# Trading places: stick-breaking branch products and the first mixer gate, with per-item rates for the weight sums

## The chip, the cores and the metric

The kernel runs on one core of one Trainium2 chip. The metric is the device time of one execution in microseconds (us). Before the change the median of 3 runs is 1070.77 us (1067.01 to 1071.44). A separate execution was recorded by the hardware profiler. The engines are PE (matrix products), PEld (its weight loads), DVE (vector engine), ACT (scalar engine), POOL (GpSimd, which here mostly issues DMAs) and SP (which issues the loads of weights).

## The reference

One decoder layer on x of 512 tokens by 1024 channels, in float32:

```python
proj = x @ w_in                      # q, k, v of three attentions, and three gates of 1024 channels
o_da = diff_attention(...)           # 4 heads, two softmax maps per head, RMSNorm per head
o_sb = stick_breaking_attention(...) # 8 heads of 64
o_dl = dilated_attention(...)        # 3 groups x 4 heads of 128
g = jax.nn.sigmoid(gates)            # 3 x 1024
merged = (g[:, :, 0] * (o_da @ w_branch_da) + g[:, :, 1] * (o_sb @ w_branch_sb)
          + g[:, :, 2] * (o_dl @ w_branch_dil))
x = layer_norm(alpha * x + merged @ w_out)
c = jnp.square(relu(x @ w_up)) @ w_down
ple = jax.nn.sigmoid(x @ w_ple_gate) * (p @ w_ple)
x = layer_norm(alpha * x + c + ple)
```

Only the order of the work around `merged`, and the time at which sums of weights are formed, are touched by the change.

## The kernel before, in words

**Products.** Every float32 operand is split into a rounded high part and a low part (fp32r), and a product is three matmuls: high x high, high x low, low x high. Some large products follow a scheme with seven products of half blocks in place of eight (`seven`, L541; `value_pair`). It needs sums and differences of blocks on both sides. Those of the activations are called forms here: `value_forms` (L343) loads x transposed again as eight `xr` tiles through POOL (L347) and makes the forms for the dilated values on DVE and ACT; `mixer_forms` (L507) makes those for the gates. Those of the weights are made by DMAs alone.

**Weights.** They are streamed in chunks of 128 x 1024 floats (512 KB): SP loads a `raw` tile (a ring of 7), ACT casts it to `wh` (L212), DVE subtracts to get `wl` (L214; rings of 6). `pump` (L220) does this a few chunks ahead of the item that uses them.

**Items.** `trunk` builds a list of 298 items in program order. An item is a group of matmuls (`mm`) into one bank of the matrix accumulator, with an evacuation (`ev`) that is issued one item later, and a `size` (a full item is a product of 128 rows by 512 with eight blocks, a half item half of that). A bank is one of two `mm` banks or one of six `at` banks. Items 1 to 64 are projections: q and k tiles ("T" items), values, and the seven-product items of `value_pair` (33 to 46). After that:

| items, before | what |
| --- | --- |
| 65 to 78 | `gate_alone(0, 1)`: gate of the stick-breaking branch, 14 half items |
| 79 to 86 | `branch_items(1)`: o_sb @ w_branch_sb, 8 half items |
| 87 to 100 | `gate_chain(1, 2)`: gate of the dilated branch |
| 101 to 108 | `branch_items(2)` |
| 109 to 122 | `gate_chain(2, 0)`: gate of the differential branch |
| 123 to 134 | `branch_items(0)`, with items that transpose `merged` between them |
| 135 to 297 | output projection, first norm, embedding, MLP (from about 173), second norm |

In a branch item a `pre` function, run one item ahead, puts the sigmoid on the gate (`gate_sig`, L495, ACT at L499); the evacuation multiplies the product by it on DVE (L651) and for branch 1 keeps the result as `merged`, for the others adds it to `merged` (L655).

**The loop** (L1816 and following) walks the items. For each it may add a generator to `pending`, may drain (L1827: ahead of item `branch_at[1] - 1`, which is 78, it steps all attention generators to their end), splits the heads' outputs two items ahead of a branch (`split_oT`, after stepping until the heads are ready), issues the previous item's evacuation, pumps weights, adds credit for sums, runs `pre`, calls `step()` and issues the matmuls.

`step()` advances the attention generators: eight `sb_head`, four `dil_head` (score products L1672, softmax over tables, a combination with L1721, transposes L1740), and sixteen `da_block(head, query block)`. A `da_block` does two score products, a softmax on ACT and DVE (L1583 to L1595), lets three steps pass, transposes (L1600), copies (`wT`, L98), and multiplies with the values (L1614). The last block of a head then normalizes (a power on POOL, `on` at L1627) and transposes once more (L1633). The bias tables of `da_block` are loaded by POOL (L1364) and copied by DVE (L1374).

**Weight sums.** 200 steps of 512 KB each combine blocks of weights in DRAM: a copy (L970) or an accumulating DMA (L968), all in POOL's queue, up to four sums taken in turn. Each step is made to wait for the weight split that was issued last. How many steps an item issues is set by a credit: 2.6 times the item's size for items 12 to 64, 1.4 times for 65 to 128, and 0.42 per item from 166 on (`RATES`). SP later loads the sums as weights.

Of the kernel before, what the change touches and what calls it, by code (L numbers as in the profile page):

```python
# [55 lines left out]
def trunk(tc, a, out):  # L56
    nc = tc.nc
    es = ExitStack()
    with es:
# [170 lines left out]
        items = []  # L230
# [164 lines left out]
        def value_pair(nv):  # L395


            v_from[0] = len(items) - 4
            cs, s, x = {}, {}, {}
            w = [a["wv"][nv + n, c].rearrange("p k n -> p (k n)") for n in range(2) for c in range(4)]  # L400

            for p in (2, 1, 7, 6, 4, 5, 3):
                for r in range(2):
                    if not r:
                        blk = {1: 0, 2: 2, 4: 6}.get(p)
                        cs[p] = [chunk(vsum[kp][{5: 0, 6: 1, 7: 2, 3: 3}[p]] if blk is None else w[blk + kp], 1024)
                                 for kp in range(2)]

                    def bank(p=p, r=r):
                        if p == 5:  # L410
                            x[r] = at_bank()
                        return x[r] if p in (5, 3) else at_bank() if r else mm_bank()

                    def mm(ps, p=p, r=r):
                        for k in range(4):
                            c = cs[p][k // 2]
                            n = slice(k % 2 * 512, k % 2 * 512 + 512)
                            h, lo = vf[p][k][r]
                            go, end = k == 0 and p != 3, k == 3 and p != 5
                            nc.tensor.matmul(ps, h, c["h"][:, n], start=go, stop=False, skip_group_check=True)  # L420
                            nc.tensor.matmul(ps, h, c["l"][:, n], start=False, stop=False, skip_group_check=True)
                            nc.tensor.matmul(ps, lo, c["h"][:, n], start=False, stop=end, skip_group_check=True)

                    def ev(ps, p=p, r=r):
                        if p in (2, 7):
                            s[p, r] = slot("dl_v")
                            nc.scalar.copy(s[p, r], ps)
                        elif p == 1:
                            s[1, r] = slot("dl_v")
                            nc.vector.tensor_add(s[2, r], s[2, r], ps)  # L430
                            nc.scalar.copy(s[1, r], ps)
                            V["dl_v", 1, r] = s[2, r]
                        elif p == 6:
                            nc.vector.tensor_add(s[1, r], s[1, r], ps)
                            nc.vector.tensor_add(s[7, r], s[7, r], s[1, r])
                        elif p == 3:
                            nc.vector.tensor_add(s[1, r], s[1, r], ps)
                            V["dl_v", 1, 2 + r] = s[1, r]
                        else:
                            o = V["dl_v", 2, r + 2 * (p == 5)] = slot("dl_v") if p == 4 else s[7, r]  # L440
                            nc.vector.scalar_tensor_tensor(o, s[7, r], -1.0, ps, op0=OP.mult, op1=OP.subtract)
                    item(cs[p] if r else [], mm, ev, need=cs[p], bank=bank, size=0.5)

        def v_items(nv, name, g):
            cs = [chunk(a["wv"][nv, c].rearrange("p k n -> p (k n)"), 1024) for c in range(4)]
            for tt in range(4):
                def mm(ps, tt=tt):
                    for k in range(8):
                        c = cs[k // 2]
                        s = slice((k % 2) * 512, (k % 2) * 512 + 512)  # L450
                        x1, x2 = xh[k][:, tt * P:tt * P + P], xl[k][:, tt * P:tt * P + P]
                        nc.tensor.matmul(ps, x1, c["h"][:, s], start=k == 0, stop=False)  # L452
                        nc.tensor.matmul(ps, x1, c["l"][:, s], start=False, stop=False)
                        nc.tensor.matmul(ps, x2, c["h"][:, s], start=False, stop=k == 7)  # L454
                        if k == 3:
                            yield

                def ev(ps, tt=tt):
                    if name == "sb_v":
                        v = [slot(name, F32R).rearrange("p (h two d) -> p h two d", two=2, d=64) for _ in range(2)]  # L460
                        pv = ps.rearrange("p (h d) -> p h d", d=64)
                        for i in range(2):
                            hs = slice(4 * i, 4 * i + 4)
                            nc.scalar.copy(v[i][:, :, 0, :], pv[:, hs, :])
                            nc.vector.tensor_sub(v[i][:, :, 1, :], pv[:, hs, :], v[i][:, :, 0, :].bitcast(F32))
                        V[name, g, tt] = v
                    else:
                        t = slot(name)
                        cp(t, ps)
                        V[name, g, tt] = t  # L470
                item(cs if tt == 3 else [], mm, ev, need=cs)

        nt, nv = 2, 0
        order = main_order()
# [15 lines left out]
        merged = {}  # L490
# [46 lines left out]
        def seven(forms, operand, bank_of, done):  # L537

            cs = {}
            for p in (2, 1, 7, 6, 4, 5, 3):  # L540
                for r in range(2):  # L541
# [19 lines left out]
                    if p == 5:  # L561
                        bank_of.get("sums", set()).add(len(items))
                    item(cs[p] if r else [], mm, ev, need=cs[p], bank=bank, size=0.5)

        msum = [[[dram.tile([P, 1024], F32, name=f"msum{n}_{m}_{i}") for i in range(4)] for m in range(2)]
                for n in range(3)]
# [67 lines left out]
        def branch_items(i, behind=()):  # L634
            behind = list(behind)
            for half in range(2):
                cs = [chunk(a["wb"][i, half, c].rearrange("p k n -> p (k n)"), 1024) for c in range(2)]
                for tt in range(4):
                    def mm(ps, tt=tt, cs=cs):
                        q = slice(tt * P, tt * P + P)  # L640
                        for k in range(4):
                            c = cs[k // 2]
                            n = slice(k % 2 * 512, k % 2 * 512 + 512)
                            h, lo = oTs[4 * i + k]
                            nc.tensor.matmul(ps, h[:, q], c["h"][:, n], start=k == 0, stop=False)  # L645
                            nc.tensor.matmul(ps, h[:, q], c["l"][:, n], start=False, stop=False)  # L646
                            nc.tensor.matmul(ps, lo[:, q], c["h"][:, n], start=False, stop=k == 3)  # L647

                    def ev(ps, tt=tt, half=half):
                        g = sg.pop((i, tt, half))  # L650
                        nc.vector.tensor_mul(g, g, ps)  # L651
                        if i == 1:
                            merged[tt, half] = g
                        else:
                            nc.vector.tensor_add(merged[tt, half], merged[tt, half], g)  # L655

                    def pre(tt=tt, half=half):
                        sg[i, tt, half] = gate_sig(i, tt, half)
                    item(cs if tt == 3 else [], mm, ev, need=cs, bank=at_bank, size=0.5)
                    items[-1]["pre"] = pre  # L660
                    if half and behind:
                        behind.pop(0)()

# [12 lines left out]
            item([], mm, ev, size=0.08)  # L676

        last_plain = len(items)
        gate_alone(0, 1)
        branch_at = {1: len(items)}  # L680
        branch_items(1)
        for n, i in ((1, 2), (2, 0)):
            gate_chain(n, i)
            branch_at[i] = len(items)
            branch_items(i, () if i else [lambda k=k: turn_item(k) for k in range(4)])

# [254 lines left out]
        def sum_steps():  # L941
# [34 lines left out]
            todo = deque(up_steps(vsum[m], [w[2 + i // 2, i % 2 * 2 + m] for i in range(4)], True) for m in range(2))  # L976
            todo.extend(up_steps(msum[n][m], a["wgm"][n, m]) for n in range(3) for m in range(2))
            todo.extend(up_steps(gsum[m], a["wg"][m]) for m in range(2))
            for m in range(ND):
                todo.append(up_steps(usum[m], a["wu"][m]))  # L980
                if m < ND - 1:
                    todo.append(down_steps(m))
            run = []
            while todo or run:
                while todo and len(run) < 4:
                    run.append(todo.popleft())
                for g in list(run):
                    s = next(g, None)
# [824 lines left out]

        DA_TABS = 44
        sum_steps_ = sum_steps()
        RATES = 2.6, 1.4  # L1816
        credit = 0.0
        plain_left[0] = last_plain
        forms_at = last_plain - 5
        freed = 8  # L1820
        prev = None
        for n, it in enumerate(items):
            if n == v_from[0]:
                pending.append(value_forms())
            if n == forms_at:
                pending.append(mixer_forms())
            if n == branch_at[1] - 1:  # L1827
                while active or waiting:
                    step()
            for i in range(3):  # L1830
# [25 lines left out]
            if n == 13:  # L1856
                pending.append(tables())

            if 12 <= n < wout_at - 6:
                credit += it["size"] * (RATES[0] if n < last_plain else RATES[1])  # L1860
            elif n > ple_at + 14:
                credit += 0.42
            while credit >= 1:
                credit -= 1
                next(sum_steps_, None)
# [139 lines left out]
```

## Time and profile before

| quantity | value |
| --- | --- |
| median of the runs shown | 1070.77 us (1067.01 to 1071.44, 3 runs) |
| the profiled execution's own time | 1073.48 us |
| its span in the trace | 1071.8 us |
| mean granted clock of PE over the span | 0.987 |
| HBM read, written | 251.21 MB, 106.98 MB |
| instructions | 15018 |

"Busy" is the share of the span in which an engine executed an instruction. A window is a stretch of the span, in us from its start; PEclk is the clock that PE was granted in it, as a part of full speed; GB/s is what the DMA engines moved. A row of the timeline is: start in us, duration in us, engine, line and operation, output and inputs with their shapes, how many instructions of the kind stand together, and, in brackets, the idle time ahead of it on its engine with the instruction that ended that. A row of the waits names the waiting engine and line, the instruction waited for, and then the total in us, the count and the longest.

### The profile page before, as it was taken

Reading aid. Unit: us, or ns where it says so; the run is one execution under the profiler, and the core shown is the slowest. Engines: PE = TensorE matmul, PEld = TensorE weight load, DVE = VectorE, ACT = ScalarE, POOL = GpSimd, SP = SyncE. Lnnn points to the kernel's source line nnn. Section 1 sums busy time; section 2 is a strip of 40 time slices with the busy share of each in tenths; the row PEclk is TensorE's granted clock in tenths of the full one; section 3 lists DMA queues with packets and bytes.
Section 4 is the critical chain, followed back from the end, with each engine's and each line's share of the span. In section 5 each row is a group of like instructions: output and inputs, shape, how many; then the busy total and the mean of one; then the engine's idle time right before and its main releaser. Section 6 shows DMA issues by size and latency. Waiting matters only on the chain.

```text
span 1071.8 us, 15018 instructions
## 1 busy us (share of the span) xinstructions
PE 1046.1 (98%) x5474; PEld 889.5 (83%) x5474; DVE 764.1 (71%) x1352; ACT 576.8 (54%) x982; POOL 179.5 (17%) x271
## 2 busy tenths in 40 slices
PE   9999999999999999898999999999999999999997
PEld 6887788878888788786888888888999989989885
DVE  6887667639864656985466664789677867877976
ACT  6675445426434544665362633585656565566741
POOL 0002322332322433021121130000111010100000
PEclk9999999998999999898999999999999999999999
DMA  8348987998999999387599993248999879857612
GB/s 312 112 168 252 230 266 204 289 311 241 362 270 256 321 267 321 115 252 266 153 289 302 320 348 101 79 125 299 262 313 285 288 220 288 270 182 240 195 41 79
DMA packets 72761, 254.32 MB, mean 237 GB/s; under 512 B 8968, under 2 KB 9880, under 8 KB 72688
## 3 DMA queue, kind: packets, MB, share of 16 engines
q0 software_dynamic: 32464, 116.21, 41.1%
q1 hardware_dynamic: 39648, 136.24, 36.4%
q8 instruction: 43, 0.70, 0.2%
q10 hardware_dynamic: 576, 0.92, 0.2%
q14 instruction: 30, 0.25, 0.1%
HBM read 251.21 MB, written 106.98 MB: 334 GB/s over the span
## 4 chain that ended last, share of the span: by engine, by line
PE 82%; DMA 10%; DVE 5%; issue 1%; ACT 1%; POOL 0%; DVEq 0%; SPq 0%; POOLq 0%; ACTq 0%
PE mm L87 8%; PE mm L89 8%; PE mm L88 8%; PE at L1131 4%; PE at L1132 4%; PE at L1133 4%; DMA msum<-in_wgm_dram 4%; PE at L552 3%; PE at L553 3%; PE at L554 3%; PE at L645 2%; PE at L646 2%; PE at L647 2%; DMA msum<-msum 2%; PE mm L452 2%; PE mm L454 2%
## 5 line engine op out<-in xcount | busy, mean ns | idle before, releaser
L214 DVE TENSOR_TENSOR wl<-raw,wh 128x1024 fp32r<-128x1024 f32 x251 | 305.5, 1223 | 135.8 <-ACT wh L212 133.6
L212 ACT CAST wh<-raw 128x1024 fp32r<-128x1024 f32 x251 | 263.3, 1051 | 253.9 <-PE mm L88 123.5
L87 PE MATMUL mm<-xhT,wh 128*128 128x512 f32 x304 | 121.1, 398 | 1.0 <-DVE da_qb L101 1.0
L89 PE MATMUL mm<-xhT,wl 128*128 128x512 f32 x304 | 119.2, 392 | 0.1
L88 PE MATMUL mm<-xlT,wh 128*128 128x512 f32 x304 | 118.9, 391 | 0.0
L1131 PE MATMUL at<-wh,hh 128*128 128x512 f32 x188 | 73.7, 392 | 0.0
L1132 PE MATMUL at<-wl,hh 128*128 128x512 f32 x188 | 73.7, 392 | 0.0
L87 PE MATMUL mm<-x1hT,wh 128*128 128x256 f32 x256 | 73.6, 288 | 0.0
L1133 PE MATMUL at<-wh,hl 128*128 128x512 f32 x188 | 73.1, 389 | 0.0
L88 PE MATMUL mm<-x1lT,wh 128*128 128x256 f32 x256 | 72.3, 283 | 0.0
L89 PE MATMUL mm<-x1hT,wl 128*128 128x256 f32 x256 | 71.8, 283 | 0.0
L87 PEld LDWEIGHTS mm<-xhT,wh 128*128 128x128 f32 x304 | 57.2, 188 | 12.7 <-PE at L1600 1.2
L89 PEld LDWEIGHTS mm<-xhT,wl 128*128 128x128 f32 x304 | 57.1, 188 | 12.6 <-DVE wl L214 0.5
L88 PEld LDWEIGHTS mm<-xlT,wh 128*128 128x128 f32 x304 | 57.1, 188 | 10.4
L87 PEld LDWEIGHTS mm<-x1hT,wh 128*128 128x128 f32 x256 | 48.8, 191 | 4.7 <-ACT up L1065 3.0
L88 PEld LDWEIGHTS mm<-x1lT,wh 128*128 128x128 f32 x256 | 48.8, 191 | 1.5
L968 POOL DMA_DIRECT2D usum<-in_wu_dram x32 | 27.8, 868 | 127.4 <-DVE wl L214 102.2
L89 PEld LDWEIGHTS mm<-x1hT,wl 128*128 128x128 f32 x256 | 48.6, 191 | 0.0
L1133 PEld LDWEIGHTS at<-wh,hl 128*128 128x128 f32 x188 | 35.3, 188 | 7.7
L1131 PEld LDWEIGHTS at<-wh,hh 128*128 128x128 f32 x188 | 35.5, 189 | 6.0
L1132 PEld LDWEIGHTS at<-wl,hh 128*128 128x128 f32 x188 | 35.5, 189 | 5.5
L968 POOL DMA_DIRECT2D dsum<-in_wd_dram x28 | 24.8, 886 | 86.4 <-DVE wl L214 72.0
(554 smaller groups left out, 2679.5 us busy)
## 6 DMA issues: line engine op xcount, KB each, us to landing
usum<-in_wu_dram POOLq DMA_DIRECT2D x48, 512.0 KB, 9.6
dsum<-in_wd_dram POOLq DMA_DIRECT2D x42, 512.0 KB, 10.6
raw<-in_wt_dram SPq DMA_DIRECT2D x38, 512.0 KB, 7.8
msum<-in_wgm_dram POOLq DMA_DIRECT2D x36, 512.0 KB, 14.2
raw<-usum SPq DMA_DIRECT2D x32, 512.0 KB, 5.3
raw<-dsum SPq DMA_DIRECT2D x28, 512.0 KB, 5.2
raw<-in_wd_dram SPq DMA_DIRECT2D x25, 512.0 KB, 4.5
raw<-msum SPq DMA_DIRECT2D x24, 512.0 KB, 7.7
```

The lines of the kernel that those rows point to most:

```text
L87: nc.tensor.matmul(ps, wh, xh, start=start, stop=False, skip_group_check=True)
L88: nc.tensor.matmul(ps, wh, xl, start=False, stop=False, skip_group_check=True)
L89: nc.tensor.matmul(ps, wl, xh, start=False, stop=stop, skip_group_check=True)
L212: i = nc.scalar.copy(h, raw)
L214: i = nc.vector.tensor_sub(lo, raw, h.bitcast(F32))
L552: nc.tensor.matmul(ps, h[:, q], c["h"][:, n], start=go, stop=False, skip_group_check=True)
L553: nc.tensor.matmul(ps, h[:, q], c["l"][:, n], start=False, stop=False, skip_group_check=True)
L554: nc.tensor.matmul(ps, lo[:, q], c["h"][:, n], start=False, stop=end, skip_group_check=True)
L968: i = nc.gpsimd.dma_start(o, i, accum_op=OP.add, max_dma_last_dim=4096)
L1131: nc.tensor.matmul(ps, h[:, q], c["h"][:, s], start=go, stop=False, skip_group_check=True)
L1132: nc.tensor.matmul(ps, h[:, q], c["l"][:, s], start=False, stop=False, skip_group_check=True)
L1133: nc.tensor.matmul(ps, lo[:, q], c["h"][:, s], start=False, stop=end, skip_group_check=True)
```

## The change

1. `branch_items(1)` comes ahead of `gate_alone(0, 1)`: items 65 to 72 are the branch products, 73 to 86 the gate. The branch items of branch 1 use an `mm` bank, have no `pre`, and their evacuation is a copy on ACT into a slot `b1`, which is `merged`.
2. The sigmoids of the first gate and the multiplication into `merged` (`first_gate`) run as the `pre` of items 89 to 96, within the second gate.
3. The drain stands ahead of item 86 (`gated_at - 1`), and `mixer_forms` is added at item 64 instead of 60.
4. The credit for sums is size times a rate of the item's kind: 2.5 for items 12 to 64, but 1.4 for values and 0.5 for `value_pair`; 1.2 for gate items, 1.5 for branch items, 1.0 otherwise, up to item 146; then 0.56 per item from item 158. The order of the sums for the MLP is written out, and at most two are taken in turn once nine or fewer are left to start.

The instructions per engine are as many as before, but for eight copies more on ACT. By item 30 the credit has issued 43 sum steps instead of 49, by item 64 92 instead of 119, by item 165 144 instead of 163; the rest follow by item 265 instead of 252.

```diff
 (value_pair)
+                    items[-1]["rate"] = 0.5
 (v_items)
+                items[-1]["rate"] = 1.4
 (seven)
+                    items[-1]["rate"] = 1.2
 (branch_items)
                     def ev(ps, tt=tt, half=half):
+                        if i == 1:
+                            t = slot("b1")
+                            nc.scalar.copy(t, ps)
+                            merged[tt, half] = t
+                            return
                         g = sg.pop((i, tt, half))
                         nc.vector.tensor_mul(g, g, ps)
-                        if i == 1:
-                            merged[tt, half] = g
-                        else:
-                            nc.vector.tensor_add(merged[tt, half], merged[tt, half], g)
+                        nc.vector.tensor_add(merged[tt, half], merged[tt, half], g)
...
-                    item(cs if tt == 3 else [], mm, ev, need=cs, bank=at_bank, size=0.5)
-                    items[-1]["pre"] = pre
+                    item(cs if tt == 3 else [], mm, ev, need=cs, bank=None if i == 1 else at_bank, size=0.5)
+                    items[-1]["rate"] = 1.5
+                    if i != 1:
+                        items[-1]["pre"] = pre
...
         last_plain = len(items)
-        gate_alone(0, 1)
+        for it in items:
+            it.setdefault("rate", 2.5)
+        def first_gate(tt, half):
+            g = gate_sig(1, tt, half)
+            nc.vector.tensor_mul(merged[tt, half], merged[tt, half], g)
+
         branch_at = {1: len(items)}
         branch_items(1)
+        gate_alone(0, 1)
+        gated_at = len(items)
         for n, i in ((1, 2), (2, 0)):
             gate_chain(n, i)
+            if n == 1:
+                for j, th in enumerate([(tt, half) for half in range(2) for tt in range(4)]):
+                    items[gated_at + 2 + j]["pre"] = lambda th=th: first_gate(*th)
             branch_at[i] = len(items)
...
-            for m in range(ND):
-                todo.append(up_steps(usum[m], a["wu"][m]))
-                if m < ND - 1:
-                    todo.append(down_steps(m))
+            for kind, m in ("u0", "u1", "d0", "u2", "u3", "d1", "d2", "u4", "u5", "d3", "d4", "u6", "u7", "d5", "d6"):
+                m = int(m)
+                todo.append(up_steps(usum[m], a["wu"][m]) if kind == "u" else down_steps(m))
             run = []
             while todo or run:
-                while todo and len(run) < 4:
+                while todo and len(run) < (4 if len(todo) > 9 else 2):
                     run.append(todo.popleft())
...
-        RATES = 2.6, 1.4
-        forms_at = last_plain - 5
+        forms_at = last_plain - 1
...
-            if n == branch_at[1] - 1:
+            if n == gated_at - 1:
                 while active or waiting:
                     step()
...
-            if 12 <= n < wout_at - 6:
-                credit += it["size"] * (RATES[0] if n < last_plain else RATES[1])
-            elif n > ple_at + 14:
-                credit += 0.42
+            if 12 <= n < wout_at + 12:
+                credit += it["size"] * it.get("rate", 1.0)
+            elif n > ple_at + 6:
+                credit += 0.56
```

## The prediction, on record before the changed kernel ran

> **What bounds the kernel now.** I read the first two parts of the page, then what PE waited for, then windows around each wait, then the timeline inside them.
>
> ```profile
> span 1071.8 us, 15018 instructions
> PE 1046.1 (98%) x5474; PEld 889.5 (83%) x5474; DVE 764.1 (71%) x1352; ACT 576.8 (54%) x982; POOL 179.5 (17%) x271
> ```
>
> PE is busy 98% of the span and the change takes no product away. So a gain can only come out of the 1071.8 - 1046.1 = 25.7 us in which PE stands still, and out of busy time that ran at a low clock. PE's waits, largest first (columns: who waits, for whom; us, count, longest):
>
> ```profile
> PE mm L420 <- ACT dl_q L285: 4.3, 1, 4.3
> PE at L1600 <- DVE lg L1595: 3.4, 2, 2.9
> PE at L1633 <- DVE on L1627: 2.7, 1, 2.7
> PE at L1614 <- DVE wT L98: 2.1, 1, 2.1
> PE at L1740 <- DVE L L1721: 1.6, 1, 1.6
> ```
>
> Five releasers, four places. The windows tell what each place costs with the low clock behind it (PE's busy time second, PEclk the granted clock):
>
> ```profile
> core 0: us, PE busy (x) PEld busy (x) DVE busy (x) ACT busy (x) POOL busy (x), PEclk, DMA share, GB/s
> 239.00:249.00 10.00, 5.71 (x17) 4.32 (x16) 8.51 (x13) 4.97 (x7) 2.04 (x4) 0.66 1.05 220
> 440.00:452.00 12.00, 8.56 (x41) 6.79 (x40) 11.81 (x29) 9.48 (x21) 0.00 (x0) 0.91 0.14 45
> 452.00:460.00 8.00, 8.00 (x33) 6.76 (x33) 5.68 (x8) 3.54 (x8) 0.52 (x1) 0.71 0.56 189
> 488.00:499.50 11.50, 6.77 (x32) 5.32 (x31) 8.81 (x13) 9.29 (x16) 3.44 (x6) 0.77 0.92 314
> 499.50:505.00 5.50, 5.50 (x16) 4.26 (x15) 0.32 (x1) 0.69 (x1) 0.00 (x0) 0.55 0.78 305
> 505.00:523.00 18.00, 18.00 (x81) 14.92 (x80) 6.77 (x9) 2.70 (x3) 0.52 (x1) 1.00 0.25 89
> ```
>
> I price a place as its waits plus busy time times (1 - clock).
>
> - A, value forms: 4.3 + 5.71 x 0.34 = 6.2 us.
> - B, the last attention blocks beside the mixer's forms: 3.4 + 8.56 x 0.09 + 8.00 x 0.29 = 6.5 us.
> - C, the drain ahead of item 78: 2.7 + 2.1 + 6.77 x 0.23 + 5.50 x 0.45 = 8.8 us.
> - D, the bias tables: 1.6 us.
>
> The sum is 23.1 us. The timeline shows how each comes about and checks the clock terms:
>
> ```profile
> 238.32 1.22 DVE L370 TENSOR_TENSOR fr<-xr,xr 128x256 f32<-128x256 f32 x2 [10.51 <-DMA xr<-in_xT_dram]
> 243.04 0.60 ACT L285 ACTIVATE dl_q<-mm 128x512 f32<-128x512 f32 x1
> 243.69 0.82 PE L420 MATMUL mm<-wh,xhT 128*128 128x512 f32 x1 [4.29 <-ACT dl_q L285]
> 248.75 1.95 PE L1672 MATMUL at<-dl_k,dl_q 128*128 128x128 f32 x16
> 445.61 1.29 DVE L521 TENSOR_TENSOR xr<-xr,xr 128x512 f32<-128x512 f32 x2
> 446.81 0.69 DVE L522 SCALAR_TENSOR_TENSOR xr<-xr,xr 128x512 f32<-128x512 f32 x1
> 449.75 0.75 DVE L1595 SCALAR_TENSOR_TENSOR lg<-lg,rr,lg 128x512 f32<-128x512 f32 x1
> 450.55 1.11 PE L1600 MATMUL at<-ident,lg 128*128 128x128 f32 x4 [2.94 <-DVE lg L1595]
> 493.99 1.84 PE L1614 MATMUL at<-da_v,wT 128*128 128x128 f32 x8 [2.07 <-DVE wT L98]
> 498.48 1.09 PE L1633 MATMUL at<-ident,on 128*128 128x128 f32 x4 [2.66 <-DVE on L1627]
> 499.22 0.78 PE L645 MATMUL at<-wh,oTh 128*128 128x512 f32 x1
> 504.48 0.40 PE L645 MATMUL at<-wh,oTh 128*128 128x512 f32 x1
> ```
>
> At A, DVE stood 10.51 us for the `xr` loads; the casts of the form are queued on ACT ahead of the evacuation L285, which frees the bank that L420 wants. At C the last block (3,3) is stepped to its end with no product between its steps: PE waits, does 1.84 us, waits again. One item of branch products is 12 matmuls: 504.48 - 499.22 = 5.26 us, against 12 x 18.00/81 = 2.67 us at the pace of 505 to 523, 2.6 us more; my clock term for that stretch says 2.5. At A likewise 248.75 - 243.69 = 5.06, 2.4 over 2.67 (term: 1.9).
>
> **The change part by part.** The counts of items and instructions are the program's, read from the code.
>
> *Order.* The 14 gate products and the 8 branch products exchange places; PE's work stays. The drain's condition now stands ahead of item 86 instead of 78. Eight further steps fall beside products (21.3 us of PE work), so block (3,3) goes one step per item and nothing is left to drain: C saves 8.8 us. What would be late next is `split_oT(1)`, 14 items earlier at item 63; it needs only the stick-breaking heads, done some thirty items before: nothing.
>
> *Later forms.* The 16 DVE operations of `mixer_forms` come four items later. At 440 to 452 DVE is busy 11.81 of 12 us, and those of them ahead of 449.75 (1.29, 0.69, 0.69 and four more of about 0.69) stand between the blocks' softmaxes and L1600. They now fall beside branch products, whose results ACT copies, not DVE. So B saves 6.5. But by my count of DVE work per item at the traced durations, items 71 to 77 then hold 26.8 us of DVE beside 24.2 us of PE. This 2.6 us is the price of a new wait; the lower end is 0, since a lead of three items of rings absorbs it, the upper end is B's own 6.5. I take 2.5, the nearest figure.
>
> *Gate later.* These rows price it:
>
> ```profile
> L499 ACT ACTIVATE graw<-graw 128x512 f32<-128x512 f32 x16 | 10.2, 635 | 9.8 <-DVE graw L620 4.9 <-DVE graw L626 3.9 <-DVE graw L623 0.9
> L618 ACT COPY graw<-at 128x512 f32<-128x512 f32 x12 | 7.0, 583 | 6.5 <-PE at L554 6.5
> L651 DVE TENSOR_TENSOR graw<-graw,at 128x512 f32<-128x512 f32 x24 | 16.4, 685 | 24.7 <-PE at L647 24.6
> 452.00:488.00 36.00, 36.00 (x174) 30.34 (x174) 30.55 (x66) 21.18 (x49) 6.92 (x10) 0.94 0.86 247
> 523.00:640.00 117.00, 117.00 (x522) 96.66 (x521) 75.21 (x87) 60.87 (x78) 26.46 (x41) 1.00 0.98 300
> ```
>
> Eight copies are added on ACT: 8 x 0.583 = 4.7 us, beside 21.3 us of products; ACT had 36 - 21.2 = 14.8 us free at 452 to 488. Eight sigmoids (8 x 0.635 = 5.1 us) and eight multiplications (8 x 0.685 = 5.5 us) move into the second gate, where DVE is busy 75.2 and ACT 60.9 of 117 us. Both are hidden: 0. Without that cover they would cost up to their own 15.3 us. The branch results now land in a bank of the pair that the gate products used; ACT must free one within an item of 2.7 us, with 0.6 us of work: 0.
>
> *Rates.* POOL issues its transfers in order, and each waits for the one eight places earlier (the releasers of these rows are such ones):
>
> ```profile
> 302.19 0.43 DVE L1374 COPY shf<-sh 128x512 f32<-128x512 f32 x1 [2.27 <-DMA sh<-rv]
> 305.48 0.43 DVE L1374 COPY shf<-sh 128x512 f32<-128x512 f32 x1 [0.78 <-DMA sh<-rv]
> 218.85 0.56 POOL L347 DMA_DIRECT2D xr<-in_xT_dram  x1 [2.25 <-DMA msum<-in_wgm_dram]
> 235.47 0.54 POOL L347 DMA_DIRECT2D xr<-in_xT_dram  x1 [1.68 <-DMA msum<-msum]
> 290.38 0.54 POOL L1364 DMA_DIRECT2D sh<-rv  x1 [1.94 <-DMA dsum<-in_wd_dram]
> ```
>
> The eight `xr` loads take from 218.85 to 235.47 because sum steps ahead of them are still moving. By the new rates seven fewer stand ahead of them in POOL's order, and those are spaced by the splits of weights. I put the last issue at 219 (bounded by a wait for PE that already ended at 216) to 231. The form must start 4.3 us sooner than 238.32, at 234: A saves 6.2 us, or in the worst case (235.47 again) nothing. I take 6.2, since most of that interval lies ahead of 231. The loads of the tables likewise come behind transfers that have landed: D saves 1.6.
>
> What the rates take from the front they give to the MLP: 56 sum steps behind item 165 instead of 37, 19 x 0.524 = 10.0 MB more. PE there is busy 319.95 of 320 us. I cost it at 0; the second rival has the other end.
>
> **Sum:** 8.8 + 6.5 + 6.2 + 1.6 - 2.5 = 20.6 us. The profiled execution took 1073.48 us, 1.7 beyond its span; it would take 1052.9. The median of the runs, 1070.77, lies 2.7 under it: 1050.2, so I say 1050.
>
> **Rivals.** *One wait stays or moves.* DVE binds in items 71 to 77 with the clock's loss behind it, or ACT's copies wait behind casts that wait for DVE, as at 243.04, or `xr` comes at 235 again. Each gives back 6 to 9 us: 1056 to 1059. For it: DVE's 30.55 of 36 us. Against: three places must all fail for more.
>
> *Slower: the MLP's transfers.*
>
> ```profile
> 740.00:1060.00 320.00, 319.95 (x2029) 289.52 (x2029) 244.66 (x328) 191.49 (x296) 28.57 (x41) 1.00 0.74 229
> dsum<-in_wd_dram POOLq DMA_DIRECT2D x42, 512.0 KB, 10.6
> ```
>
> 320 us x 229 GB/s = 73.3 MB; with 10.0 more, 83.3. If this stage cannot move more than it does, 83.3 / 229 = 364 us, 44 more: 1050 + 44 = 1094. It decides from 83.3 / 320 = 260 GB/s down. Also, the last sums of `dsum` are read nine items (some 23 us) after issue, by my count, where before it was 14; that binds when a step takes twice the 10.6 us of the row. Against: 523 to 640 moved 300 GB/s with PE full.
>
> *The change doesn't do what it says:* `xr` late again, the drain's waits turning up beside other products and new DVE waits taking the rest: within 5 us of 1071.
>
> *The low clock is not of the gaps' making.* At C the gaps are 2.07 and 2.66 us with work between, at B 2.94; yet the clock falls to 0.55 and 0.71. If something that stays lowers it, the clock terms of B and C (0.8 + 2.3 + 1.6 + 2.5 = 7.1) stay: saving 13.5, 1057. The starts at 499.22 right behind the gap speak against. The Trainium skill, "TensorE: Matmul & The Clock Gate", Part 1, is on this rival's side: it has the clock halved after an idle window of about 3.4 us, which no gap of B or C fills; by that rule the sum would be those 13.5 us. The trace disagrees: gaps shorter than that are followed by half pace.
>
> **How the numbers follow.** All four places go, with up to 4 us either way: 0.60 (1046 to 1054). No new wait and a further loss gone: 0.06 (1040 to 1046). One wait stays or moves: 0.17. The clock stays low: 0.05. No change: 0.05. Slower in the MLP: 0.07. A measurement of this kernel can tell 0.5%, 5.4 us, from no change. Faster: 0.60 + 0.06 + 0.17 + 0.05 = 0.88; same 0.05; slower 0.07. The range 1044 to 1062 leaves out the MLP case, no change and half of the better case, 0.15.
>
> **What would show it.** Right: no wait of PE at L420, L1600, L1614 and L1633 over 1 us, a clock of 1.00 where it now reads 0.55 to 0.91, the last `xr` issued by 231, no bare stretch ahead of the second gate. Wrong: PE waiting for `b1` copies or for `graw` in items 65 to 86 (no cover on ACT or DVE), the wait of L420 unchanged (queue), or PE idle in the MLP behind casts that wait for `raw<-dsum` (transfers).

## The result, and the profile after

| | before | after |
| --- | --- | --- |
| median of the runs, first chip | 1070.30 us (4 runs, 1067.01 to 1071.44) | 1053.44 us (4 runs, 1051.62 to 1053.94) |
| the same on another chip | 1070.09 us (9 runs) | 1051.86 us (5 runs, 1051.11 to 1053.58) |
| profiled execution, own time | 1073.48 us | 1053.37 us |
| its span | 1071.8 us | 1051.3 us |

The ratio is 0.9844 with a 95% interval of 0.9819 to 0.9869, on the other chip 0.9832 (0.9816 to 0.9848): faster by 14 to 20 us. Forecast were 1050 us and a range of 1044 to 1062. The page of the changed kernel opens:

```profile
span 1051.3 us, 15027 instructions
PE 1038.0 (99%) x5474; PEld 884.2 (84%) x5474; DVE 765.5 (73%) x1352; ACT 581.5 (55%) x990; POOL 177.8 (17%) x271
```

PE's idle time went from 25.7 to 1051.3 - 1038.0 = 13.3 us, 12.4 less. Its busy time, for the same 5474 matmuls, went from 1046.1 to 1038.0: 8.1 us, near the 9.1 that the prediction's clock terms add up to. The waits of PE (who, for whom: us, count, longest):

```profile
PE at L1325 <- DVE zero L1322: 1.3, 1, 1.3
PE mm L87 <- DVE da_qb L101: 1.0, 1, 1.0
PE at L131 <- ACT da_ka L122: 0.8, 2, 0.6
PE mm L648 <- DVE da_klb L101: 0.8, 1, 0.8
PE at L1713 <- DVE r L1706: 0.6, 1, 0.6
PE mm L420 <- ACT dl_v L427: 0.5, 1, 0.5
PE at L131 <- ACT da_kb L124: 0.3, 1, 0.3
```

The five large rows of before (L420, L1600, L1633, L1614, L1740; L1600 is L1616 now) are gone, or at L420 shrunk to 0.5 us with another releaser. The first two rows were there before. New are the rows of L648 and of `da_kb` at L131 (that of `da_ka` has grown from 0.2 us), and a remainder at L420 and L1713, which is place A. The windows that answer to those of before:

```profile
core 0: us, PE busy (x) PEld busy (x) DVE busy (x) ACT busy (x) POOL busy (x), PEclk, DMA share, GB/s
237.00:260.00 23.00, 21.86 (x102) 19.63 (x101) 21.27 (x58) 14.61 (x32) 1.08 (x2) 1.00 0.53 156
300.00:320.00 20.00, 19.87 (x123) 17.45 (x122) 12.04 (x55) 8.22 (x24) 0.00 (x0) 1.00 0.01 3
415.00:437.00 22.00, 20.36 (x112) 16.96 (x111) 17.87 (x48) 15.54 (x34) 7.65 (x11) 1.00 0.83 228
437.00:452.00 15.00, 15.00 (x83) 12.48 (x82) 10.78 (x32) 8.97 (x25) 0.84 (x2) 1.00 0.45 162
452.00:490.00 38.00, 38.00 (x187) 31.88 (x186) 32.95 (x59) 27.52 (x53) 5.32 (x8) 1.00 0.55 199
490.00:505.00 15.00, 15.00 (x70) 12.43 (x69) 13.09 (x17) 10.21 (x13) 1.65 (x2) 1.00 0.94 243
740.00:1040.00 300.00, 300.00 (x1882) 270.68 (x1881) 228.34 (x307) 178.71 (x277) 36.37 (x53) 1.00 0.81 258
```

From 437 to 505, where B and C stood, PE is busy without a gap at full clock. From 415 to 437 it now stands 1.6 us. In the MLP it is full, beside 258 GB/s instead of 229. The timeline of after shows the two remainders, first A (POOL and DVE), then the new wait (ACT and PE):

```profile
229.04 0.54 POOL L347 DMA_DIRECT2D xr<-in_xT_dram  x1 [3.27 <-PE at L1571]
```

```profile
232.71 0.61 DVE L370 TENSOR_TENSOR fr<-xr,xr 128x256 f32<-128x256 f32 x1 [5.62 <-DMA xr<-in_xT_dram]
```

```profile
415.53 2.19 ACT L237 CAST oTh<-oT 128x512 fp32r<-128x512 f32 x4
418.73 0.60 ACT L122 CAST da_ka<-da_ka 64x512 fp32r<-64x512 f32 x1
419.38 0.38 PE L131 MATMUL at<-da_ka,da_qa 128*128 128x256 f32 x1 [0.59 <-ACT da_ka L122]
```

The last `xr` load is issued at 229.04 (before: 235.47), now held up by the matmul that reads its buffer's old content. The form starts at 232.71 instead of 238.32, early enough for all but 1.1 us. At 415.53 the four casts of the split, moved here from item 77, stand on ACT ahead of the evacuation and the cast of a k projection, `da_ka`.

### The profile page after: what moved, and what is told of

It reads as the page before. It is cut to its first block, busy times and chain, and to the rows that moved or that the text cites. A ratio compares the mean times of both kernels' runs of the same rounds, so it can differ in the third digit from the quotient of the medians.

```text
span 1051.3 us, 15027 instructions
## 1 busy us (share of the span) xinstructions
PE 1038.0 (99%) x5474; PEld 884.2 (84%) x5474; DVE 765.5 (73%) x1352; ACT 581.5 (55%) x990; POOL 177.8 (17%) x271
## 3 DMA queue, kind: packets, MB, share of 16 engines
HBM read 251.21 MB, written 106.98 MB: 341 GB/s over the span
## 4 chain that ended last, share of the span: by engine, by line
PE 90%; DVE 4%; DMA 3%; ACT 2%; issue 1%; POOL 0%; DVEq 0%; ACTq 0%; POOLq 0%
PE mm L87 9%; PE mm L88 8%; PE mm L89 8%; PE at L1147 4%; PE at L1148 4%; PE at L1149 4%; PE at L554 3%; PE at L555 3%; PE at L556 3%; PE mm L453 2%; PE mm L455 2%; PE mm L454 2%; DMA msum<-in_wgm_dram 2%; PE at L89 1%; PE at L87 1%; PE at L88 1%
## 5 line engine op out<-in xcount | busy, mean ns | idle before, releaser
L212 ACT CAST wh<-raw 128x1024 fp32r<-128x1024 f32 x251 | 262.9, 1050 | 234.7 <-PE mm L88 125.6
```

Source lines behind the costliest of these rows:

```text
L212: i = nc.scalar.copy(h, raw)
```

## The experiments

Each run was compared with the kernel before on its own chip: medians of before were 1071.05 (first four runs), 1069.94 (next four) and 1070.09 (last four).

**Order alone (e1).** The changed kernel with the old rates and sums:

```diff
-            for kind, m in ("u0", "u1", "d0", "u2", "u3", "d1", "d2", "u4", "u5", "d3", "d4", "u6", "u7", "d5", "d6"):
-                m = int(m)
-                todo.append(up_steps(usum[m], a["wu"][m]) if kind == "u" else down_steps(m))
+            for m in range(ND):
+                todo.append(up_steps(usum[m], a["wu"][m]))
+                if m < ND - 1:
+                    todo.append(down_steps(m))
...
-                while todo and len(run) < (4 if len(todo) > 9 else 2):
+                while todo and len(run) < 4:
...
+        RATES = 2.6, 1.4
...
-            if 12 <= n < wout_at + 12:
-                credit += it["size"] * it.get("rate", 1.0)
-            elif n > ple_at + 6:
-                credit += 0.56
+            if 12 <= n < wout_at - 6:
+                credit += it["size"] * (RATES[0] if n < last_plain else RATES[1])
+            elif n > ple_at + 14:
+                credit += 0.42
```

> The change without its fourth part: products, first gate, drain and forms as in the changed kernel, but the rates, the order and the number of the sums taken in turn as before. Theory (four places that do not depend on each other): B and C go, 6.5 + 8.8, and the new waits of 1.6 us at the split of the stick-breaking heads are there; A (PE at L420 behind the late xr) and D stay. 1070.3 - 13.7 = 1056.6, 1055 to 1059. Rival (the fewer sum steps relieve the queues and engines everywhere, so the rates bring most of it): 1064 to 1070.

Measured: 1059.45 us (4 runs), ratio 0.9892 (0.9875 to 0.9909), 11.6 us under before, half a microsecond above the expected range. B and C are gone, the new waits at L131 and L648 are there, and so is A:

```profile
PE mm L420 <- ACT dl_q L285: 5.9, 1, 5.9
```

**Rates alone (e2).** The kernel before with the new rates, order of sums and number in turn (the same lines the other way round).

> The kernel before with the fourth part alone: rates, order of the sums, two in turn at the end. Theory: A and D go but for the 1.1 us that the changed kernel still waits at A; B and C stay with their waits at L1600, L1614 and L1633. By the profiled execution 1070.3 - 6.7 = 1063.6; if A cost less in the median execution than in the profiled one (which was 3.2 us over the median), 1064 to 1067. Rival (rates bring most): 1054 to 1058. Rival (the MLP pays for the moved sums): above 1070.

Measured: 1063.61 us (4 runs), ratio 0.9927 (0.9908 to 0.9946), 7.4 us under before. A is down to 1.1 us and D is gone; B and C stand as before (line numbers of this kernel):

```profile
PE at L1605 <- DVE lg L1600: 3.4, 2, 2.9
PE at L1638 <- DVE on L1632: 3.1, 1, 3.1
PE at L1619 <- DVE wT L98: 2.1, 1, 2.1
```

The two halves give 11.6 + 7.4 = 19.0 us, the whole 16.9 to 18.2. Within the intervals they add up, so no run here shows that one half needs the other, and the order is worth the larger part by these medians. Of the three parts of this half only the rates can have moved A and D: the first sum of the MLP is issued at 333 us, in this run as in the changed kernel, behind both places, so their order and number had not come into play.

**The drain back at item 78 (e3).** The changed kernel with

```diff
-            if n == gated_at - 1:
+            if n == gated_at - 9:
```

> The changed kernel with the drain ahead of item 78 instead of 86, one number changed. Theory: the last block still has some eight steps to go at item 78, they run bare, and C is back: two waits of PE of 2 to 3 us, then a granted clock of 0.55 to 0.8 for 5 to 15 us; 1053.4 + 8.8 = 1062, 1059 to 1064. Rival one (the new order alone leaves nothing to drain at 78): 1053, no wait. Rival two (the low clock is not made by the gaps): the waits are back with a clock near 1.00, 1057 to 1058.

Measured: 1054.68 us (4 runs), ratio 0.9848 (0.9831 to 0.9864), that is 0.4 to 1.7 us over the changed kernel by the ratios. Neither my theory nor a rival: two waits are back, but shorter, and no cold stretch follows. Waits, then windows:

```profile
PE at L1649 <- DVE on L1643: 1.4, 1, 1.4
PE mm L554 <- ACT graw L594: 1.3, 1, 1.3
```

```profile
474.00:480.00 6.00, 4.65 (x27) 3.82 (x26) 4.94 (x7) 4.17 (x8) 0.52 (x1) 1.00 0.69 252
480.00:484.00 4.00, 2.58 (x14) 1.89 (x13) 1.46 (x3) 1.19 (x3) 1.04 (x1) 1.00 0.04 15
484.00:490.00 6.00, 6.00 (x28) 4.92 (x28) 5.00 (x6) 4.63 (x6) 1.42 (x3) 1.00 0.38 129
```

PE stands 1.35 + 1.42 = 2.8 us here. (A's remainder of 1.1 us was absent in this execution, as in some others of the new rates, which hides part of it in the total.) So a drain ahead of item 78 does not cost 8.8 us by itself. I supposed the split of item 77 to be what made it dear, and tried it:

**The split early, in the kernel before (e9a).**

```diff
-                if n == branch_at[i] - 2:
+                if n == branch_at[i] - (16 if i == 1 else 2):
```

> The kernel before with the split of the stick-breaking heads at item 63 instead of 77, one number changed; order, drain and rates stay. Theory (new, from the run with the drain at 78): the bare steps alone cost little; C was dear because the split's four pairs, the gate's sums and two weight splits stood in the queues of DVE and ACT ahead of wT, scr and on: 1071 - 5 = 1066, 1064 to 1068, the waits at L1614 and L1633 near 1.4 each and the clock behind them near 1. Rival (the old step of mine: bare steps are the cause): 1069 to 1072, both waits as before.

Measured: 1069.38 us (10 runs), ratio 0.9996 (0.9980 to 1.0012): no difference, so the rival held and this theory fell. C's waits only go from 4.8 to 4.5 us, and the moved work opens a new one at 449 us:

```profile
PE at L1633 <- DVE on L1627: 2.7, 1, 2.7
PE mm L552 <- ACT graw L587: 1.8, 1, 1.8
PE at L1614 <- ACT wh L212: 1.4, 1, 1.4
PE at L1614 <- DVE wT L98: 0.4, 1, 0.4
```

**The drain late, in the kernel before (e9b).**

```diff
-            if n == branch_at[1] - 1:
+            if n == branch_at[1] + 7:
```

> The kernel before with the drain ahead of item 86 instead of 78, one number changed; order, split and rates stay. Theory: with a product beside each step the queues' length does not stop PE; C goes whole: 1071 - 8.8 = 1062, 1060 to 1065. Rival (the long queues at item 77 stop PE whether it is drained or not): 1066 to 1071, with PE waiting for DVE or ACT at 490 to 505.

Measured: 1062.31 us (4 runs), ratio 0.9931 (0.9909 to 0.9954): 7.6 us less, by one number. C is gone whole, and the wait of B is unchanged (window, then wait):

```profile
486.00:506.00 20.00, 20.00 (x97) 16.48 (x96) 13.94 (x19) 11.68 (x19) 3.63 (x7) 1.00 0.82 304
```

```profile
PE at L1600 <- DVE lg L1595: 3.4, 2, 2.9
```

So the drain's place did cause C in the old order. What it costs differs with the order: 4.8 us and a cold clock in the old one, 2.8 us at full clock in the new one. One candidate is the eight sigmoids of the first gate, which in the old order are issued into the drain too, seven of them between 493.2 and 497.9 on ACT. The row of `scr`, the first operation behind the products with the values, speaks against it: ACT stood idle ahead of it until PE was done, so no sigmoid held it up in this execution. (In the second one ACT has no idle time there and the gap is 3.06 us instead of 2.66, so some 0.4 us may have been lost in queues.)

```profile
495.92 0.28 ACT L1618 ACTIVATE scr<-at 128x128 f32<-128x128 f32 x1 [0.52 <-PE at L1614]
```

The rows of the last block in the run with the drain at 78 show another difference (its L1630 and L1649 are L1614 and L1633 of before, whose rows at 493.99 and 498.48 stand in the prediction):

```profile
478.54 1.05 PE L1630 MATMUL at<-da_v,wT 128*128 128x128 f32 x8
482.17 0.66 PE L1649 MATMUL at<-ident,on 128*128 128x128 f32 x4 [1.42 <-DVE on L1643]
```

From the end of the products with the values to the last transposes the block takes 482.17 - 478.54 - 1.05 = 2.6 us here and 498.48 - 493.99 - 1.84 = 2.7 us in the old order. The step ahead of it, from the transposes to those products, takes about 3.1 and 3.2 us. The block is no faster, but PE has more to do between its steps: of the twelve matmuls of gate item 78, seven stand in the first stretch and five in the second here, against five and none in the old order. The shorter gaps are then not followed by a low clock. Why the matmuls were placed so was not isolated.

**The forms back at item 60 (e4).** The changed kernel with `forms_at = last_plain - 5`.

> The changed kernel with the mixer's forms pending at item 60 instead of 64, one number changed. Theory: the forms' DVE work stands ahead of the last blocks' softmaxes again, PE waits about 3 us at their transposes and runs cold behind it: 1053.4 + 6.5 = 1060, 1057 to 1061. Rival (the order alone relieved DVE there, since the branch products have no DVE evacuation): 1052 to 1055, PE waits under 1 us there.

Measured: 1057.22 us (4 runs), ratio 0.9876 (0.9857 to 0.9894), about 3.8 us over the changed kernel by the medians. The size is that of my theory's lower end, the place is another: PE does not wait at the transposes but for the bank that ACT should free, with the copy to `b1` standing behind the form's cast (which waited 2.81 us for DVE). Wait, then the window behind it:

```profile
PE mm L648 <- ACT b L655: 3.2, 1, 3.2
```

```profile
441.00:449.00 8.00, 7.68 (x33) 6.39 (x34) 5.58 (x15) 3.87 (x12) 0.00 (x0) 0.79 0.01 3
```

That is the mechanism of the forecast's first rival, ACT's copies behind casts that wait for DVE, once forms and branch products meet.

**The branch copies on DVE (e8).**

```diff
-                            nc.scalar.copy(t, ps)
+                            nc.vector.tensor_copy(t, ps)
```

> The changed kernel with the eight copies of the branch products on DVE (8 x 0.69 = 5.5 us) instead of ACT (8 x 0.58), one word changed. Theory of the prediction (DVE has no slack in items 65 to 78): PE waits for banks there and pays 3 to 8 us, 1056 to 1061. Rival (the lead of the rings and the gate items behind take it up, as no wait was seen there after the change): 1052 to 1055.

Measured: 1055.52 us (4 runs), ratio 0.9863 (0.9847 to 0.9880), 3.7 us over the unaltered changed kernel of the same chip. That lies between the two forecasts, half a microsecond under the theory's range. DVE is short of time in the gate items, as I had counted: the softmax of a last block comes late again, and the clock from 470 to 490 us is 0.91.

```profile
PE at L1616 <- DVE lg L1611: 2.2, 1, 2.2
PE mm L648 <- DVE b L655: 0.7, 1, 0.7
```

**More transfers in the MLP (e5).** The changed kernel with 33 copies of 512 KB that nothing reads (excerpt; each also waits for a weight split, as the sums do):

```diff
+            if n > ple_at + 14 and n < len(items) - 12:
+                extra += 0.28
+                while extra >= 1:
+                    extra -= 1
+                    i = nc.gpsimd.dma_start(spare[n % 4], a["wgm"][0, 0, 0].rearrange("p k n -> p (k n)"), max_dma_last_dim=4096)
...
```

> The changed kernel with 33 further copies of 512 KB (17.6 MB) from one weight block into unused buffers, spread over items 166 to 285 in POOL's queue; they compute nothing. Theory: the MLP's 258 GB/s rises to about 315, as much as other stretches move with PE full, and PE stays full: 1053 to 1055. Rival (the moved sums already bring the MLP to its limit): the copies cost what they take, 17.6 MB at 258 GB/s = 68 us if nothing overlaps, and PE waits for chunks; anything over 1058 speaks for it.

Measured: 1051.90 us (4 runs), ratio 0.9835 (0.9812 to 0.9859): nothing lost. The stage moves 310 GB/s and PE has no gap:

```profile
740.00:1040.00 300.00, 300.00 (x1880) 270.54 (x1880) 227.99 (x307) 177.54 (x274) 51.20 (x82) 1.00 0.90 310
```

The second rival, a limit at 260 GB/s, is refuted: the page of this run has 268.51 MB read against 251.21, so the copies add 17.3 MB (33 x 0.524, not 17.6).

**The split four items earlier (e6).** The changed kernel with `branch_at[i] - (6 if i == 1 else 2)`.

> The changed kernel with the split of the stick-breaking heads four items earlier, at item 59, one number changed. Theory: the 4 casts on ACT and 4 subtractions on DVE (2.2 and 2.5 us) at 415 to 419 hold up the evacuation of the last k projection there; earlier they stand beside plain projections, and the waits of PE at L131 and L648 (0.85 + 0.8) go: 1.6 us less, 1051 to 1053. Rival (those waits are the projection's own chain of two casts and two subtractions, as at its other heads, and the split only stands beside): no change, 1053 to 1054, same waits.

Measured: 1050.87 us (5 runs, 1049.78 to 1052.93), ratio 0.9827 (0.9806 to 0.9849); against 0.9844 and 0.9832 of the changed kernel this alone cannot be told from no change. The trace shows about half of the expected gain: the wait at L131 falls from 0.8 + 0.3 to 0.2, that at L648 stays, as the rival had it (it is the projection's own chain).

```profile
PE mm L648 <- DVE da_klb L101: 0.7, 1, 0.7
PE at L131 <- ACT da_ka L122: 0.2, 1, 0.2
```

**A version that beats both (best, after_again).** The split at item 59, and the `xr` loads two items earlier with the forms in place:

```diff
-        WAIT = 5
+        WAIT = 7
...
-            v_from[0] = len(items) - 4
+            v_from[0] = len(items) - 6
...
-                if n == branch_at[i] - 2:
+                if n == branch_at[i] - (6 if i == 1 else 2):
```

> The changed kernel with the split of the stick-breaking heads at item 59 and the eight xr loads two items earlier (value_forms pending six items ahead instead of four, seven steps let pass instead of five, so the forms stay in place): the waits at L131 and the last 1.1 us at A go, about 2 us less than the changed kernel, 1049 to 1052. Rival: the xr buffers come free no earlier, since the buffers that they take over are read by the stick-breaking products until 228.9, so that A's rest stays: within 1 us of the changed kernel.

> The changed kernel unaltered, to be compared with the next one on one chip, and a second execution of it in the profile: 1051 to 1055, PE's wait for the late xr forms between 0 and 1.2 us.

Measured on one chip: 1050.02 us (4 runs, 1049.81 to 1050.31) against 1051.86 (5 runs, 1051.11 to 1053.58) of the unaltered changed kernel; ratios to before 0.9814 (0.9799 to 0.9828) and 0.9832. The runs do not overlap. How much of the 1.8 us belongs to the earlier loads is not shown: the profiled execution of the unaltered kernel had no remainder at A (PE busy 22.98 of 23 us at 237 to 260), and it stood 1.5 us at L308 within the first 9 us of the span, where this one stood 0.2. The rival on the buffers fell: two items earlier the loads take over other buffers, the last is issued at 213.50, and the form starts at 224.22 with no wait for it (POOL, then DVE):

```profile
213.50 0.54 POOL L347 DMA_DIRECT2D xr<-in_xT_dram  x1 [2.47 <-ACT dl_q L285]
```

```profile
224.22 1.15 DVE L370 TENSOR_TENSOR fr<-xr,xr 128x256 f32<-128x256 f32 x2
```

**The kernel before once more (before_again).**

> The kernel before unaltered, a second execution in the profile: if the 3 us by which the first profiled execution lay over its median are its own, this one lies nearer to 1070 with the waits at L1600, L1614 and L1633 unchanged, and differs at A (the xr loads) or at the start. Rival: the profiler adds them to every execution of this kernel, 1073 again.

Measured: 1069.96 us, span 1068.3: its own 3.5 us less than the first profiled execution. The waits at A, B and C are much the same (4.6 us; 3.4; 3.1 and 2.1), that at D is not; I had looked for the difference at A or at the start:

```profile
PE mm L420 <- ACT dl_q L285: 4.6, 1, 4.6
PE at L1633 <- DVE on L1627: 3.1, 1, 3.1
PE at L1740 <- DVE L L1721: 0.5, 1, 0.5
```

What differs most is the clock behind the same gaps. First the stretch behind B and that around C in this execution, then C in the first one (its row behind B, with 0.71, is in the prediction):

```profile
452.00:460.00 8.00, 8.00 (x41) 6.79 (x41) 6.92 (x13) 4.14 (x9) 1.88 (x3) 0.94 0.73 240
486.00:506.00 20.00, 14.86 (x62) 11.75 (x61) 9.42 (x14) 9.19 (x16) 2.75 (x5) 0.83 0.70 259
```

```profile
486.00:506.00 20.00, 15.27 (x59) 12.07 (x58) 11.43 (x18) 11.98 (x22) 4.34 (x7) 0.74 0.84 305
```

Behind B, 8.00 x (0.94 - 0.71) = 1.8 us; around C, 15.27 x 0.26 - 14.86 x 0.17 = 1.4; at D 1.1. Less 0.7 for longer gaps at A and C, that makes 3.6 of the 3.5 us.

## Why the prediction was right, point by point

The forecast of the likeliest case came true: direction, the mechanism at A to D and, within 0.4%, the time. Term by term, in the profiled executions; "saved" is the forecast's price less what the changed kernel still shows there, not a measurement of the term by itself:

| term | forecast, us | saved, us | from |
| --- | --- | --- | --- |
| A | 6.2 | 5.1 | 23.00 - 21.86 = 1.1 left at 237 to 260, clock 1.00 |
| B | 6.5 | 6.5 | no gap at 437 to 452 |
| C | 8.8 | 8.8 | no gap at 452 to 505 |
| D | 1.6 | 1.5 | 0.13 left at 300 to 320 |
| new wait | -2.5 | -1.6 | 22.00 - 20.36 at 415 to 437 |
| sum | 20.6 | 20.3 | spans: 1071.8 - 1051.3 = 20.5 |

The prices themselves belong to one execution of the kernel before. By the rows of its second one A costs 4.6 + 5.73 x 0.34 = 6.5 us, B 3.4 + 8.59 x 0.10 + 8.00 x 0.06 = 4.7, C 5.14 + 14.86 x 0.17 = 7.7 and D 0.5: 19.4 together, and 17.6 without the 1.8 that the second execution of the changed kernel still shows. That is near the 18.2 between the medians of that chip, and C's 7.7 near the 7.6 that moving the drain alone brought.

- **Where it was 2 to 3 us off.** The step that failed is the last one of the sum, "the median of the runs, 1070.77, lies 2.7 under it: 1050.2". I let the 2.7 us by which the profiled execution lay over the median stay with the kernel. But the changed kernel's profiled execution has 1053.37 and its median is 1053.44. The second execution of before shows why: in that pair of executions the excess lay in the clock behind B and C and in D, in the very places that the change removes. The sum made against the profiled execution gave 1052.9, and that held; the gain against the medians is the smaller one, 16.9 to 18.2.
- **A, "I take 6.2, since most of that interval lies ahead of 231".** The last load came at 229.04, within the interval, and the form at 232.71, ahead of the 234 asked for; still 1.1 us of PE's time was left in this execution, at two later waits (L420 and L1713). In others of the new rates it was near 0. The interval's lower end was wrong: a wait for PE, which I took to be over by 216, holds the last load until 229.04; with other buffers, in the best version, it was issued at 213.50. The run with the rates alone shows that they are what moves A and D.
- **B, "So B saves 6.5".** Right for the first profiled execution; 4.7 in the second. By the medians about 3.8 us hang on the forms' later place, and with the forms early the wait takes another form, ACT's copy behind a cast. That the new order alone spares the rest is inferred from the difference.
- **C, "nothing is left to drain: C saves 8.8".** Right for the move as made, and 7.6 by the drain alone in the old order. What it left unsaid is that the price was the old order's: at the same item 78 in the new order the drain costs 2.8 us, with twelve matmuls instead of five between the block's last steps.
- **The new wait, "items 71 to 77".** The size was near by luck, for the wait forecast and the wait found have nothing in common. No wait is to be seen in those items: 452 to 490 is full. The lower end given, 0, was the right one, though no run shows that the lead of the rings is the reason. That little is left the run with the copies on DVE shows: 5.5 us more on DVE cost 3.7.
- **`split_oT(1)`, "nothing".** This was the miss of place: I asked only whether the heads are ready, not what the four casts and four subtractions push back. They push back the evacuation of a k projection and cost 0.9 of the 1.6 us, by the waits of the run with the split four items earlier.
- **Gate later, "both are hidden: 0".** Held. Those multiplications are even issued from 478.9, some nine items ahead of where the list asks for them, and PE does not wait (durations min/median/max in ns, first and last start):

```profile
L690 DVE TENSOR_TENSOR b<-b,graw x8: 683/686/694, 478.9 to 506.2; 128x512 f32<-128x512 f32 x8
```

- **The MLP at 0.** Held. What the moved sums did change is the landing of the loads beside them, 7.7 us instead of 5.2 for `raw<-dsum`, and PE does not wait for it:

```profile
raw<-dsum SPq DMA_DIRECT2D x28, 512.0 KB, 7.7
```

- **The clock rival.** It fell: with the gaps gone, the clock is 1.00 in every window where it had been 0.55 to 0.91, and in the kernel before with the drain moved it is 1.00 at C alone, while it stays low behind B (0.87 at 452 to 460).

## What to carry to other kernels

When an engine is nearly full, price each of its gaps as the wait plus the busy time behind it times the missing clock, and ask of every place how much independent work stands between the steps of the chain that PE waits for; the same drain cost three times as much where five matmuls stood there instead of twelve, and a low clock followed. A moved step brings its whole train of casts and copies to the new place, so look there for the evacuation that it delays. And do not carry the offset between one profiled execution and the median over to the changed kernel: where it lies in the very stalls that go, it goes with them.

## What the runs showed of the hardware that was not expected

The low clock follows gaps that are shorter, and less exactly, than I took it. Two gaps of 1.35 and 1.42 us within 8 us (drain at 78) and one of 1.6 us (D before) left the clock at 1.00; one of 3.15 us (forms at 60) was followed by 0.79; the pair at B, 0.5 and 2.9 us, by 0.71, 0.94 and 0.87 in three executions of kernels with the same gaps (before twice, and the drain late). At C the eight matmuls of L1614 took 1.84 us behind a gap of 2.07 us in one execution and 1.13 behind one of 2.08 in the other; in the run with the drain at 78, with matmuls ahead of them, they took 1.05.

The Trainium skill, "TensorE: Matmul & The Clock Gate", Part 1, has the clock halved after an idle window of about 3.4 us, and the window is free-running: it does not restart when a kernel starts. A free-running window would allow for different clocks behind equal gaps, though no run here shows that it is the reason. The 3.4 us do not fit, since at C a gap of 2.07 us was followed by matmuls that took 1.84 us instead of 1.05. In these runs the gaps of B, C and the forms at 60 cost 1.4 to 1.9 times their own length, and single gaps up to 1.6 us just their length.

Transfers had more room than I allowed for: 310 GB/s over 300 us beside a PE without a gap, while the loads `raw<-dsum` took 10.2 us to land in the median, against 5.2 in the kernel before and 7.7 in the changed one.
